# Hybrid attention block on one core: transposes of the probabilities issued in groups

## The chip, the cores and the metric

One Trainium2 chip, one of its cores. The metric is device time in microseconds (us) of one execution of the kernel, as the median of several executions.

## The reference

One layer of a decoder on a sequence of 512 rows of width 1024, in float32. The input is normalised to `h`; one wide product `h @ w_in` gives queries, keys, values and gates of two attention branches, and the columns of two merge gates.

- Differential attention, 4 heads: two score matrices of 512 x 512 per head (64 wide each), causal mask, softmax on each, and the weights `a0 - lam * a1` times values 128 wide; then an RMS norm and a SiLU gate.
- MoBA attention, 8 heads of 64; with blocks of 256 and a top-3 of at most two blocks it is plain causal softmax attention here, followed by a SiLU gate.

```python
a = jax.nn.softmax(s, axis=-1)
w = a[:, :, 0] - lam * a[:, :, 1]
return jnp.einsum('bhqk,bkhe->bqhe', w.astype(v.dtype), v)
```

Both branches are projected to 1024, merged by sigmoid gates, projected once more and added to `x`; a gated per-layer embedding is added, and a last RMS norm gives the output.

## The kernel before, in words

Every float32 product is made of three (or two) products of a rounded high part and a rest: `hi` is made by ScalarE (ACT) with a copy, `lo` by a subtraction `src - hi` on VectorE (DVE) or GpSimd (POOL). `mm3` (L114) issues the three matmuls.

**The clock of the program.** The order of the instructions on every engine is written out by a small scheduler that runs while the kernel is built. `tick` (L68) advances a counter and resumes every running generator whose time has come, the oldest first. `spawn` (L65) adds a generator, with `after` ticks of delay; a generator that yields `n` sleeps for `n` ticks. The long matrix products call `step` (L213) after each group of matmuls on TensorE (PE): three matmuls of 512 columns in `proj_T`, six of 256 columns in `proj_v`. So one tick is about one group of matmuls, and what the generators issue in a tick lands in the instruction streams between two such groups. Engines run their own streams in order and wait on semaphores for each other; a tick fixes places in the streams, not times.

**The heads.** For `j` from 0 to 7 the loop at L605 computes values (`proj_v`, 8 ticks), then `project(j)`: keys, queries and gate of pair `j`, 8 ticks each, and spawns `attention` for them two ticks later. `j` 0 to 3 are the differential heads (`kind` 0), `j` 4 to 7 hold two MoBA heads each (`kind` 1). So the attention of head `j` is issued in the middle of the products of head `j + 1`. Counted from the end of `project(j)`, the key product of the next head ends with tick 16, its query product with tick 24, its gate product with tick 32, and the next attention starts at tick 34.

**Attention.** `PLAN` (L35) is a list of steps by hand for the four query tiles of 128 rows: `S` issues the score matmuls (L482, L484) into two banks of PSUM, `E` the masked maximum on DVE (L492) and the exponentials on ACT (L497), `N` the normalisation on DVE (L502 and L534, L535, or L532), `T` the transposes of the normalised probabilities on PE (L508); a number is a sleep in ticks. For tile `i` there are `i + 1` blocks of 128 x 128 to transpose, into one bank of the tag `tp` (two banks, taken in turn). One tick later ACT copies the tile's transposed blocks to `pth`, and again one tick later DVE computes `ptl` (both by `split_later`, L102 and L104). After the last tile the product with the values is issued: L566 to L568 with `mm3` for a differential head (bank `av`), L557 to L560 for the MoBA pair. For a differential head there follow the square on ACT (L572), the gate product `o` on DVE (L573), row sums (L577) and a broadcast of the norm (L583).

With the ticks counted as above, a plan begins at tick 2 and reaches `T0` (with `S3`) at tick 9, `T1` at 15, `N3` at 19, `T2` at 20, `T3` at 24 and the product with the values at 29.

**What stands beside it.** When the key product of the next head has ended, `qk_tile` (L432) begins at tick 17: four operations of rotary embedding on DVE (L435 to L438), at tick 21 two copies to `ks` on ACT (L443), at 22 two more to the other half (L447), at 23 two subtractions to `kl` on DVE (L454), at 24 two copies of them (L458). For the queries the same begins at tick 25 with the four operations on DVE; the copies to `qs` (L443) come at tick 29 and the two subtractions to `qs` (L454) at tick 31, behind L573 of the head before. The next head's first scores (L482) read `qs`. Weights are split by `pump_split` (L179) every third tick: the copy `wh` or `vh` on ACT (L102), `wl` or `vl` on POOL (L104).

Of the kernel before, what the change touches and what calls it, by code (L numbers as in the profile page):

```python
# [9 lines left out]
F32 = mybir.dt.float32  # L10
F32R = mybir.dt.float32r
I32 = mybir.dt.int32
AF = mybir.ActivationFunctionType
ALU = mybir.AluOpType

P = 128
S = 512
D = 1024
NT = S // P
# [12 lines left out]
PUMP = 3  # L32
AV_LAG = 1
BUFS = dict(w=3, v=2)
PLAN = "S0 E0 2 S1 1 E1 1 N0 S2 3 E2 N1 T0 S3 5 E3 1 N2 T1 4 N3 1 T2 4 T3 5"  # L35
SUB_LAG = (2, 3, 1, 2, 3)
C_DQ, C_DK, C_DV, C_DG, C_MQ, C_MK, C_MV, C_MG, C_GA, C_GB = (
    0, 512, 1024, 1536, 2048, 2560, 3072, 3584, 4096, 5120)
# [3 lines left out]
def hybrid_block(ctx, tc, x, p, norm_g, w_in, lq1, lk1, lq2, lk2, subln_g, w_bd, w_bm,  # L42
                 w_out, w_ple, w_pg, final_g, rope, out):
    nc = tc.nc
    V, A, G, T, Y = nc.vector, nc.scalar, nc.gpsimd, nc.tensor, nc.sync
# [12 lines left out]
    def bank(tag):  # L58
        return ps.tile([P, 512], F32, tag=tag, name=tag, bufs=BANKS[tag])
# [5 lines left out]
    def spawn(gen, after=0):  # L65
        running.append([clock[0] + after, gen])
# [34 lines left out]
    def split_later(hi, lo, src, gap=1, eng=None):  # L101
        A.activation(hi, src, AF.Copy)  # L102
        yield gap
        (eng or V).tensor_sub(lo, src, hi.bitcast(F32))  # L104

    def pow_half(ssum, n, eps, cols):

        v = small.tile([P, cols], F32, name=f"rv{cols}")
        y = small.tile([P, cols], F32, name=f"ry{cols}")
        V.tensor_scalar(v, ssum, 1.0 / n, eps, op0=ALU.mult, op1=ALU.add)  # L110
        G.tensor_tensor(out=y, in0=v, in1=mhalf[:, :cols], op=ALU.pow)  # L111
        return y

    def mm3(acc, ahi, alo, bhi, blo, start, stop):  # L114
        T.matmul(acc, ahi, bhi, start=start, stop=False)  # L115
        T.matmul(acc, ahi, blo, start=False, stop=False)  # L116
        T.matmul(acc, alo, bhi, start=False, stop=stop)  # L117
# [156 lines left out]
    with tc.tile_pool(name="norm", bufs=2) as npool:  # L274
# [32 lines left out]
        pts = [bank("tp") for _ in range(2)]  # L307
# [194 lines left out]
            V.reciprocal(self.rc, self.sm)  # L502
            return self.rc

    def p_transposed(e, i):
        acc = bank("tp")
        for kb in range(i + 1):
            T.transpose(acc[:, kb * P:(kb + 1) * P], e[:, kb * P:(kb + 1) * P], ident)  # L508
        return acc[:, :(i + 1) * P].rearrange("p (k q) -> p k q", q=P)

    def pt_tiles():

        return (att.tile([P, 13 * P], F32R, name="pth"), att.tile([P, 13 * P], F32R, name="ptl"))

    def pt_q(pt, i):
        v = pt.rearrange("p (b q) -> p b q", q=P)
        return v[:, i:4 * i + 1:3]

    def pt_k(pt, kb):
        return pt[:, 4 * kb * P:(3 * kb + NT) * P]  # L520

    def attention(kind, j, qkg, v):

        q, k, g = qkg
        sm = [Softmax(q, k, i) for i in range(NT)]
        pts = [pt_tiles() for _ in range(1 + kind)]

        def norm(i):
            e, rc = sm[i].e, sm[i].recip()
            if kind:  # L530
                for s in range(2):
                    V.tensor_scalar(e[s], e[s], rc[:, s:s + 1], 0.5, op0=ALU.mult, op1=ALU.mult)  # L532
            else:
                V.tensor_scalar(e[1], e[1], rc[:, 1:2], nlam, op0=ALU.mult, op1=ALU.mult)  # L534
                V.scalar_tensor_tensor(e[0], e[0], rc[:, 0:1], e[1], op0=ALU.mult, op1=ALU.add)  # L535

        def trans(i):
            for s in range(1 + kind):
                acc = p_transposed(sm[i].e[s], i)
                spawn(split_later(pt_q(pts[s][0], i), pt_q(pts[s][1], i), acc), after=1)  # L540

        for op in PLAN.split():
            if op[0] == "S":
                sm[int(op[1])].scores()
            elif op[0] == "E":
                sm[int(op[1])].exps()
            elif op[0] == "N":
                norm(int(op[1]))
            elif op[0] == "T":
                trans(int(op[1]))  # L550
            else:
                yield int(op)
        if kind:
            for s in range(2):
                acc = bank(("av", "tp")[s])
                vp = v.rearrange("p (t h e) -> p t h e", t=NT, h=4)[:, :, 2 * (j % 2) + s]
                for kb in range(NT):  # L557
                    for n in range(2):
                        T.matmul(acc[:, kb * P:], vp[:, kb], pt_k(pts[s][n], kb), start=kb == 0 and n == 0,
                                 stop=kb == NT - 1 and n == 1)  # L560
                spawn(moba_out(j, s, acc, g[0], sm[3].e[s]), after=1)
                yield AV_LAG
            return
        acc = bank("av")
        vp = v.rearrange("p (t h n e) -> p t h n e", t=NT, h=2, n=2)[:, :, j % 2]
        for kb in range(NT):  # L566
            mm3(acc[:, kb * P:], vp[:, kb, 0], vp[:, kb, 1], pt_k(pts[0][0], kb), pt_k(pts[0][1], kb),
                kb == 0, kb == NT - 1)  # L568
        yield SUB_LAG[0]

        sq = sm[3].e[0]
        A.activation(sq, acc, AF.Square)  # L572
        V.scalar_tensor_tensor(oraw[j], acc, gsub, g[0], op0=ALU.mult, op1=ALU.mult)  # L573
        yield SUB_LAG[1]
        tot = bank("tp")
        for i in range(NT):
            T.matmul(tot[:, 2 * i:2 * i + 2], sq[:, i * P:(i + 1) * P], ones, start=True, stop=True)  # L577
        yield SUB_LAG[2]
        rstd = pow_half(tot[:, 0:2 * NT:2], P, SUBLN_EPS, NT)
        yield SUB_LAG[3]  # L580
        rb = bank("tp")
        for i in range(NT):
            T.transpose(rb[:, i * P:(i + 1) * P], rstd[:, i:i + 1].to_broadcast([P, P]), ident)  # L583
        yield SUB_LAG[4]
        V.tensor_mul(oraw[j], oraw[j], rb)

    def moba_out(j, s, acc, g, tmp):
        own, other = slice(s * HD, (s + 1) * HD), slice((1 - s) * HD, (2 - s) * HD)
        A.activation(tmp[own], acc[other], AF.Copy)
        yield 1  # L590
        V.tensor_add(tmp[own], acc[own], tmp[own])
        G.tensor_mul(oraw[4 + j][own], tmp[own], g[own])
# [12 lines left out]
    for j in range(7):  # L605
        if j:
            h = (j + 1) // 2
            if j % 2:
                vs.append(v_tile())
            proj_v(vs[h], h // 2, h % 2, (0, 1) if j % 2 else (2, 3))  # L610
        spawn(attention(j // 4, j % 4, project(j), vs[j // 2]), after=2)
    acc = bank("pj")
    proj_T(acc, ("a", 0))
    A.activation(oraw[7], acc, AF.Copy)
    spawn(attention(1, 3, project(7), vs[3]), after=2)

    first = [ropet[:, 0], ropet[:, 1]]
    acc = bank("pj")  # L620
# [49 lines left out]
    for m in range(3, 8):  # L670
        sig = []
        for n in range(2):
            acc = bank(("pj", "sc")[n])
# [183 lines left out]
```

## Time and profile before

| | us |
|---|---|
| median of 3 runs | 493.42 (493.4 to 493.52) |
| profiled execution | 493.49 |
| its span, first to last instruction | 491.3 |
| PE busy / DVE / ACT / POOL | 479.3 / 294.2 / 244.2 / 118.2 |
| instructions | 6677 |

The profiled execution takes 2.2 us beside its span, and it is 0.07 us above the median. The mean granted TensorE clock is 0.997 of full speed. Busy time of PE is the union of its instructions, and matmuls overlap, so the distance between two starts tells more than a duration: in a steady stream a matmul of 512 columns starts 0.23 us after the one before.

### The profile page before, as it was taken

The page shows a single profiled execution, that of the slowest core. Times are in us where ns is not written, and L with a number is a line of the kernel's source. Part 1 is how long each engine was busy: PE and PEld are TensorE (multiplying, and loading weights), DVE is VectorE, ACT ScalarE, POOL GpSimd, SP SyncE. Part 2 cuts the span into 40 slices and gives each one's busy share as a digit, 9 for nine tenths or more (in the row PEclk, how much of TensorE's full clock was granted, in tenths as well). Part 3 has the DMA queues.
Part 4 walks back from the last instruction along what each step waited for, and adds up shares of the span by engine and source line. Part 5 has one row for each costly group of instructions (what it writes and reads, how often), then busy time and mean ns, then how long its engine had stood idle before and what let it go on. Part 6 is the DMA issues. An engine that isn't in the chain of part 4 may idle for free.

```text
span 491.3 us, 6677 instructions
## 1 busy us (share of the span) xinstructions
PE 479.3 (98%) x2485; PEld 408.1 (83%) x2485; DVE 294.2 (60%) x626; ACT 244.2 (50%) x521; POOL 118.2 (24%) x104
## 2 busy tenths in 40 slices
PE   7999999999999999999999999999999999999994
PEld 5898988889888898988888887888888888888884
DVE  3775685877858668677686547642354245353565
ACT  3865755575645657556676545422332232332442
POOL 1105543542344423425456440000000000000001
PEclk9999999999999999999999999999999999999998
DMA  8954331232114311211323312423322293200013
GB/s 266 340 177 128 97 119 44 85 97 76 45 43 121 94 45 43 87 31 57 87 86 102 113 45 85 129 85 87 128 86 87 88 326 100 85 1 0 1 43 128
DMA packets 63007, 47.73 MB, mean 97 GB/s; under 512 B 2304, under 2 KB 56320, under 8 KB 62976
## 3 DMA queue, kind: packets, MB, share of 16 engines
q1 hardware_dynamic: 62832, 47.06, 31.3%
q8 instruction: 19, 0.31, 0.3%
q10 hardware_dynamic: 144, 0.26, 0.1%
q14 instruction: 12, 0.10, 0.1%
HBM read 45.22 MB, written 2.10 MB: 96 GB/s over the span
## 4 chain that ended last, share of the span: by engine, by line
PE 84%; DVE 9%; ACT 2%; issue 1%; DMA 1%; SPq 0%; POOL 0%; POOLq 0%; DVEq 0%; ACTq 0%
PE pj L115 15%; PE pj L117 14%; PE pj L116 14%; PE sc L115 4%; PE sc L116 4%; PE sc L117 4%; PE av L116 3%; PE tp L115 3%; PE tp L116 3%; PE tp L117 3%; PE av L117 3%; PE av L115 3%; PE sc L484 2%; PE sc L482 2%; DVE ptl L104 2%; PE tp L508 2%
## 5 line engine op out<-in xcount | busy, mean ns | idle before, releaser
L104 POOL TENSOR_TENSOR wl<-raw,wh 128x512 fp32r<-128x512 f32 x54 | 71.7, 1342 | 96.9 <-ACT wh L102 96.6
L115 PE MATMUL pj<-hThi,wh 128*128 128x512 f32 x232 | 93.0, 401 | 0.0
L117 PE MATMUL pj<-hThi,wl 128*128 128x512 f32 x232 | 90.8, 392 | 0.0
L116 PE MATMUL pj<-hTlo,wh 128*128 128x512 f32 x232 | 90.6, 390 | 0.0
L102 ACT ACTIVATE wh<-raw 128x512 fp32r<-128x512 f32 x96 | 56.8, 623 | 20.1 <-PE tp L117 17.2
L111 POOL TENSOR_TENSOR ry<-rv,mhalf 128x1 f32<-128x1 f32 (+1 forms) x11 | 8.2, 742 | 233.4 <-DVE rv L110 233.4
L497 ACT ACTIVATE sc<-sc,nm 128x128 f32<-128x128 f32 (+3 forms) x64 | 35.5, 556 | 33.2 <-DVE nm L492 33.2
L117 PEld LDWEIGHTS pj<-hThi,wl 128*128 128x128 f32 x232 | 43.6, 188 | 9.5
L104 DVE TENSOR_TENSOR wl<-raw,wh 128x512 fp32r<-128x512 f32 x42 | 27.8, 687 | 38.7 <-ACT wh L102 38.5
L116 PEld LDWEIGHTS pj<-hTlo,wh 128*128 128x128 f32 x232 | 43.7, 188 | 7.9
L115 PEld LDWEIGHTS pj<-hThi,wh 128*128 128x128 f32 x232 | 43.7, 188 | 7.8
L115 PE MATMUL pj<-vh,hThi 128*128 128x256 f32 (+1 forms) x136 | 39.8, 293 | 0.0
L492 DVE CUSTOM_DVE_ANT_0 sc<-sc,mask 128x128 f32<-128x128 f32 (+3 forms) x64 | 28.8, 487 | 18.4 <-PE sc L484 18.4
L117 PE MATMUL pj<-vh,hTlo 128*128 128x256 f32 (+1 forms) x136 | 39.0, 287 | 0.0
L116 PE MATMUL pj<-vl,hThi 128*128 128x256 f32 (+1 forms) x136 | 39.0, 287 | 0.0
L104 DVE TENSOR_TENSOR ptl<-tp,pth 128x128 fp32r<-128x128 f32 (+3 forms) x48 | 22.0, 486 | 23.9 <-ACT pth L102 23.8
L104 DVE TENSOR_TENSOR vl<-raw,vh 128x512 fp32r<-128x512 f32 x28 | 18.6, 687 | 29.0 <-ACT vh L102 29.0
L102 ACT ACTIVATE vh<-raw 128x512 fp32r<-128x512 f32 x48 | 28.4, 626 | 12.9 <-issue 8.6
L104 POOL TENSOR_TENSOR vl<-raw,vh 128x512 fp32r<-128x512 f32 x20 | 25.9, 1307 | 25.6 <-ACT vh L102 25.6
L102 ACT ACTIVATE pth<-tp 128x128 fp32r<-128x128 f32 (+3 forms) x48 | 19.0, 430 | 16.9 <-PE tp L508 16.7
L116 PEld LDWEIGHTS pj<-vl,hThi 128*128 128x128 f32 x136 | 25.9, 191 | 0.5
L115 PEld LDWEIGHTS pj<-vh,hThi 128*128 128x128 f32 x136 | 25.9, 190 | 0.5
(285 smaller groups left out, 1066.7 us busy)
## 6 DMA issues: line engine op xcount, KB each, us to landing
raw<-in_w_in_dram SPq DMA_DIRECT2D x48, 512.0 KB, 3.9
raw<-in_w_out_dram SPq DMA_DIRECT2D x8, 512.0 KB, 3.8
raw<-in_w_ple_gate_dram SPq DMA_DIRECT2D x8, 512.0 KB, 3.7
xt<-in_x_dram SPq DMA_DIRECT2D x4, 512.0 KB, 8.5
raw<-in_w_branch_diff_dram SPq DMA_DIRECT2D x8, 256.0 KB, 2.9
raw<-in_w_branch_moba_dram SPq DMA_DIRECT2D x8, 256.0 KB, 3.2
xs<-in_x_dram SPq DMA_DIRECT2D x1, 2048.0 KB, 10.8
out_dram<-o SPq DMA_DIRECT2D x3, 512.0 KB, 2.6
```

Of the source, the lines that this page charges most:

```text
L102: A.activation(hi, src, AF.Copy)
L104: (eng or V).tensor_sub(lo, src, hi.bitcast(F32))
L111: G.tensor_tensor(out=y, in0=v, in1=mhalf[:, :cols], op=ALU.pow)
L115: T.matmul(acc, ahi, bhi, start=start, stop=False)
L116: T.matmul(acc, ahi, blo, start=False, stop=False)
L117: T.matmul(acc, alo, bhi, start=False, stop=stop)
L482: T.matmul(self.accs[s][:, :kv], qs_[:, s, qs], ks_[:, s, :kv], start=True, stop=False)
L484: T.matmul(self.accs[s][:, :kv], qs_[:, s, qs], kl[:, s, :kv], start=False, stop=True)
L492: V.tensor_tensor_reduce(out=self.e[s], in0=self.accs[s][:, :kv], in1=mask[:, 384 - i * P:384 - i * P + kv], op0=ALU.add, op1=ALU.min, sca ...
L497: A.activation(self.e[s], self.e[s], AF.Exp, bias=self.nm[:, s:s + 1], scale=-1.0, accum_out=self.sm[:, s:s + 1])
L508: T.transpose(acc[:, kb * P:(kb + 1) * P], e[:, kb * P:(kb + 1) * P], ident)
```

## The change

The transposes of tiles 0 and 1 are issued together (`T01`), at the place of `T1`, into one bank: three blocks. For differential heads tiles 2 and 3 are issued together as well (`T23`), at tick 23, that is three ticks after the old place of `T2` and one before that of `T3`. Their seven blocks are more than the four that fit in a bank, so each of the two gets a bank of its own. The copies of a bank's tiles are issued in one tick, their subtractions in the next. MoBA pairs keep `T2` and `T3` where they were. The product with the values stays at tick 29. The number of instructions is the same; a differential head takes three banks for its transposes instead of four, a MoBA pair six instead of eight.

```diff
-PLAN = "S0 E0 2 S1 1 E1 1 N0 S2 3 E2 N1 T0 S3 5 E3 1 N2 T1 4 N3 1 T2 4 T3 5"
+PLAN = ("S0 E0 2 S1 1 E1 1 N0 S2 3 E2 N1 S3 5 E3 1 N2 T01 4 N3 4 T23 6",
+        "S0 E0 2 S1 1 E1 1 N0 S2 3 E2 N1 S3 5 E3 1 N2 T01 4 N3 1 T2 4 T3 5")
...
-    def p_transposed(e, i):
-        acc = bank("tp")
+    def p_transposed(acc, e, i):
+
         for kb in range(i + 1):
...
+        def split_tiles(s, tiles):
+            for i, acc in tiles:
+                A.activation(pt_q(pts[s][0], i), acc, AF.Copy)
+            yield 1
+            for i, acc in tiles:
+                V.tensor_sub(pt_q(pts[s][1], i), acc, pt_q(pts[s][0], i).bitcast(F32))
+
-        def trans(i):
+        def trans(*group):
+
             for s in range(1 + kind):
-                acc = p_transposed(sm[i].e[s], i)
-                spawn(split_later(pt_q(pts[s][0], i), pt_q(pts[s][1], i), acc), after=1)
-
-        for op in PLAN.split():
+                acc, at, tiles = bank("tp"), 0, []
+                for i in group:
+                    if at + i + 1 > NT:
+                        spawn(split_tiles(s, tiles), after=1)
+                        acc, at, tiles = bank("tp"), 0, []
+                    tiles.append((i, p_transposed(acc[:, at * P:], sm[i].e[s], i)))
+                    at += i + 1
+                spawn(split_tiles(s, tiles), after=1)
+
+        for op in PLAN[kind].split():
...
-                trans(int(op[1]))
+                trans(*map(int, op[1:]))
```

## Rows read from the trace of the kernel before

**Rows 1.** The page, busy time by engine.
```profile
PE 479.3 (98%) x2485; PEld 408.1 (83%) x2485; DVE 294.2 (60%) x626; ACT 244.2 (50%) x521; POOL 118.2 (24%) x104
```
**Rows 2.** The waits: waiter, releaser, us in total, times, longest.
```profile
PEld av L116 <- DVE ptl L104: 2.6, 4, 0.8
```
**Rows 3.** Timeline of PE: start, us, instruction; `T2` of head 0, `T3` of head 4.
```profile
68.91 0.49 PE L508 MATMUL tp<-ident,sc 128*128 128x128 f32 x3
...
69.48 0.39 PE L116 MATMUL pj<-hTlo,wh 128*128 128x512 f32 x1
69.71 0.40 PE L117 MATMUL pj<-hThi,wl 128*128 128x512 f32 x1
...
191.22 1.04 PE L508 MATMUL tp<-ident,sc 128*128 128x128 f32 x8
...
192.33 0.40 PE L116 MATMUL pj<-hTlo,wh 128*128 128x512 f32 x1
```
**Rows 4.** Timeline of PE: value product's first matmul and the next product's, heads 0, 1.
```profile
75.88 0.39 PE L115 MATMUL av<-pth,v 128*128 128x512 f32 x1
...
78.35 0.45 PE L115 MATMUL pj<-hThi,wh 128*128 128x512 f32 x1
...
105.63 0.39 PE L115 MATMUL av<-pth,v 128*128 128x512 f32 x1
...
107.87 0.45 PE L115 MATMUL pj<-hThi,wh 128*128 128x512 f32 x1
```
**Rows 5.** Timelines of ACT and DVE, head 1, between `T2` and the value product.
```profile
100.26 0.49 ACT L102 ACTIVATE pth<-tp 128x384 fp32r<-128x384 f32 x1
...
103.87 0.64 ACT L102 ACTIVATE wh<-raw 128x512 fp32r<-128x512 f32 x1
104.40 0.58 ACT L102 ACTIVATE pth<-tp 128x512 fp32r<-128x512 f32 x1
...
102.69 0.74 DVE L435 STREAM_SHUFFLE qr<-pj 128x512 f32<-128x512 f32 x1
...
105.40 0.68 DVE L104 TENSOR_TENSOR ptl<-tp,pth 128x512 fp32r<-128x512 f32 x1
```
**Rows 6.** Timelines of ACT, DVE and PE, head 1, up to head 2's first scores.
```profile
108.07 0.60 ACT L572 ACTIVATE sc<-av 128x512 f32<-128x512 f32 x1 [0.70 <-PE av L117]
...
108.70 0.75 DVE L573 SCALAR_TENSOR_TENSOR o<-av,gsub,gate 128x512 f32<-128x512 f32 x1 [2.62 <-ACT sc L572]
109.48 1.41 DVE L454 TENSOR_TENSOR qs<-pj,qs 64x512 fp32r<-64x512 f32 x2
...
112.23 0.42 PE L482 MATMUL sc<-ks,qs 128*128 128x128 f32 x2
```
**Rows 7.** Timelines of DVE and ACT, head 0, the same places.
```profile
60.99 0.29 DVE L104 TENSOR_TENSOR ptl<-tp,pth 128x128 fp32r<-128x128 f32 x1 [0.26 <-ACT pth L102]
...
70.19 0.75 DVE L535 SCALAR_TENSOR_TENSOR sc<-sc,rc,sc 128x512 f32<-128x512 f32 x1
...
73.16 0.75 DVE L435 STREAM_SHUFFLE qr<-pj 128x512 f32<-128x512 f32 x1
...
73.74 0.58 ACT L102 ACTIVATE pth<-tp 128x512 fp32r<-128x512 f32 x1
...
78.55 0.60 ACT L572 ACTIVATE sc<-av 128x512 f32<-128x512 f32 x1 [1.36 <-PE av L117]
```
**Rows 8.** Timelines of DVE and PE, head 4 (MoBA): subtractions of `T1`, `T3`, value product.
```profile
184.77 0.76 DVE L104 TENSOR_TENSOR ptl<-tp,pth 128x256 fp32r<-128x256 f32 x2 [2.27 <-ACT pth L102]
...
195.25 1.28 DVE L104 TENSOR_TENSOR ptl<-tp,pth 128x512 fp32r<-128x512 f32 x2
...
195.99 0.50 PE L559 MATMUL av<-ptl,v 128*128 128x512 f32 x1
```
**Rows 9.** Timelines of PE and DVE, start of the kernel: transposes and first reads.
```profile
7.32 1.11 PE L311 MATMUL tp<-ident,praw 128*128 128x128 f32 x4 [2.08 <-DMA praw<-in_p_dram]
...
8.05 1.51 DVE L366 CAST pTh<-tp 128x256 fp32r<-128x256 f32 x4 [8.05 <-PE tp L311]
```

## The prediction

> **What bounds the kernel now.** First the page's busy times: PE is busy for 98% of the span [rows 1], so only what shortens PE's own stream or removes one of its waits gains anything, and every new wait of PE costs its full length. Then the waits: the only ones of PE between the start and the merge come from the rest `ptl` of the probabilities, and it is the weight loads of the value product that show them, four times, once per differential head [rows 2]. Then the timelines of one differential head (its successor repeats it, with small differences between even and odd heads) and of one MoBA pair.
>
> **The change part by part.**
>
> *The grouping itself.* From the start of a group of transposes to the second matmul behind it, less one ordinary matmul of 0.23 us (69.48 to 69.71): three transposes take 0.57 - 0.23 = 0.34 us, eight take 192.33 - 191.22 - 0.23 = 0.88 us [rows 3]. That is 0.11 us each at either size, with nothing fixed per group. So a group of 3 or 7 takes PE what its parts took: 0.
>
> *The differential value product.* In head 0 it takes 78.35 - 75.88 = 2.47 us, in head 1 107.87 - 105.63 = 2.24 us; heads 2 and 3 repeat these [rows 4]. Without a wait it is three matmuls each of 512, 384, 256 and 128 columns: 0.23 us for the first size and about 0.1 for the last, as for a transpose [rows 3], with 0.18 and 0.12 by columns between them, 1.87 us in all. The loss is 0.60 and 0.37 us, in four heads 1.95 us. It comes from the order on DVE: the last `ptl` (tick 26) stands behind the four query operations of tick 25. With `T23` at tick 23 both subtractions are issued at tick 25 ahead of those four, since their generator is older. When would the last one be done, in head 1? ACT: the copy of tile 2 is no longer ahead of the key copies (0.39 us earlier: 0.49 less 0.1 of overlap); the weight split of 103.87 now stands behind instead of ahead (0.53 earlier); the key chain is 0.37 later (next paragraph). So tile 2's copy starts at 104.40 - 0.39 - 0.53 + 0.37 = 103.85, tile 3's at 104.24 and ends at 104.82, and `ptl` of 0.68 ends at 105.5 [rows 5]. It is needed at 105.63 + 0.23 = 105.86. In head 0, where ACT has no split there, I get 75.4 against 76.1. The wait goes in all four heads: **-1.95 us**. Its cover is 0.3 to 0.7 us.
>
> *`T01` on ACT and DVE.* Tile 0's copy and subtraction move from tick 10/11, where DVE had time, to 16/17, directly ahead of the key operations, which then run on DVE without a pause. In a differential head the subtractions begin later by the extra copy and last longer by the extra subtraction, of 0.29 us [rows 7], about 0.21 with its overlap; the copy, of the same size, I take at 0.16. Together 0.37 us, if both subtractions wait for both copies of the bank. The trace speaks for that: DVE's gate product `o` waited 2.62 us for ACT's square, though both only read the bank [rows 6], and at the start DVE's first cast, of columns transposed long before, waited until 8.05 for transposes at 7.32 into other columns of the bank [rows 9]. So waits follow banks, not columns. The Trainium skill has the rule behind it (PSUM — Partial Sum Buffer, "PSUM bank collisions raise a hardware error"): guard a bank, not an address, because two engines on different columns of one bank collide too. The trace agrees in both rows; by columns the shift would be about 0.15 us in place of 0.37.
>
> *MoBA.* Four copies and four subtractions in place of two each (one pair: 0.76 us at `T1` [rows 8]). The transposes begin 0.22 us earlier, as `T0` no longer precedes `S3`, but a bank is complete only after three; I get the key operations starting 0.45 us later (between 0.1, by columns, and 0.5). From there DVE and ACT hand each other the chain of keys, `T2` and queries up to `ptl` of `T3`, 195.25 to 195.9, and the value product starts its second matmul at 195.99 [rows 8]: nothing in between absorbs it. Pairs 4, 5 and 6 have this; pair 7 has no next queries. 3 x 0.45 = **+1.35 us**.
>
> *The new wait: the query operations.* They now stand behind both subtractions, and these behind the key copies. In head 1 they start at 105.45 instead of 102.69 [rows 5]: 2.76 us late. Behind them in order: `qs` copies, a split, the square on ACT, `o` and the subtractions to `qs` on DVE. Of the lateness the square absorbs 0.70 us, which ACT waited for PE; 2.06 us remain, and the subtractions end at 109.48 + 1.41 + 2.06 = 112.95 [rows 6]. Head 2's first scores were due at 112.23, now 0.37 earlier; the second of them, 0.13 later, reads the second half of `qs`: due at 111.99, with a weight load ahead of it. Wait: 1.1 us, in heads 1 and 3 **+2.2 us** (0.5 to 1.6 each, if the overlaps of 0.1 per instruction fall out more or less well). In head 0 the queries start at 75.3 instead of 73.16, 2.1 late, and the square had 1.36 us to spare [rows 7]: 0.8 remains, and the same sum leaves the scores late by 0.1 us at most.
>
> *`T3`'s input.* `N3` ended at 70.94 in head 0 [rows 7], now at 71.31. PE reaches tick 23 three groups after 68.91 [rows 3], at 70.97, and tile 3 at 71.3, its first weight load 0.15 us sooner: a wait of 0.2 us at most, which then delays the scores too instead of adding to their wait. Heads 0 and 2 together **+0.4 us**; in heads 1 and 3 the normalisation ends 0.1 sooner than needed.
>
> *Costed at nothing.* `S3` starts 0.11 us sooner, its maxima too; DVE then idles until `T1`. Banks of `tp`: each is read long before its third use. POOL's subtractions follow the splits that ACT now issues up to 2.8 us later behind `qs`; the weights are used two products on, some 11 us, so only a shift of that size would show. SP's loads follow the splits, six tiles ahead. After pair 7 everything is as before.
>
> *Sum.* -1.95 + 1.35 + 2.2 + 0.4 = +2.0 us on the profiled execution's 493.49 us, which is 0.07 us above the median: 495.4 us.
>
> **The rivals.**
>
> *The query chain has more slack than I count.* If head 2's scores are never late (the lateness must shrink by 1.1 us, or the scores be later by as much), -1.95 + 1.35 + 0.4 = -0.2 is left: 493.2 us. For it: I follow seven instructions on two engines, each good to 0.1 us. Against it: DVE's order is fixed by the program, and the idle time in rows 6 is what it is.
>
> *The waits follow columns.* Then `T01` shifts the keys by 0.15 us, MoBA's product by 0.1 to 0.2, the scores wait 0.85 us: -1.95 + 1.7 + 0.45 = +0.2, 493.6 us. Rows 6 and 9 speak against it.
>
> *Faster: only the value product changes.* The one mechanism is the first `ptl` wait going, with slack in the keys' chain for `T01` and in the queries' chain for `T23`: -1.95 to -1.0, about 491.9 us. It decides if the subtractions to `qs` end before 111.8 in head 1, that is if the queries start less than 1.6 us late. What speaks for it is that every displaced operation runs on engines that are idle 40 to 50% of the span; what speaks against it is that DVE has no gap in the places named.
>
> *The change does not do what it says.* For tiles 2 and 3 it does not: they get two banks, merely issued together. That is in the sum.
>
> *The rule on rotating banks.* If the copies of a bank could not begin until its whole group is through, and this held up PE at the next use of the bank, each `T01` would cost up to its copies, 0.4 us, times 7: +2.8, with the value product's gain +0.9 and 494.3 us. But the bank's next use is five ticks on, 3.4 us, while the copies and subtractions end some 2 us after the group. The Trainium skill says this of independent groups (Perfetto Trace Analysis, "Optimizing Tensor Performance", Matmuls): rotate them through banks, so that one is evacuated while the next is computed. No row here shows PE waiting for a bank.
>
> **How the numbers follow.** A measurement of this kernel tells about 0.2%, 1 us, from no change. Chances: the forecast, with its own spread of 494.5 to 496.5, 0.55; more slack in the query chain 0.14; columns 0.10; faster 0.15; rotation or others 0.06. Slower by over 0.2% (above 494.4): 0.57, the forecast and a little of the last. Within 0.2%: 0.27. Faster: 0.16. The forecast's own range is 494.5 to 496.5; down to 492.5 it takes in the columns, the slack and part of the faster case, and upward it ends at 496.4, with the waits of heads 1 and 3 at 1.6 us.
>
> **What the changed kernel's profile would show.** The wait of the value product's weight loads for `ptl` should be gone from the list for L116; the twelve matmuls should take 1.9 us in all four heads. In its place PE's weight loads should wait at L482 for DVE's L454 in heads 1 and 3, about 1 us each, and DVE should stand idle for over 1 us ahead of the subtractions of `T23`, with the query operations behind. In pairs 4 to 6 the second matmul of the value product should start 0.45 us later after the first. The prediction is wrong if the scores do not wait, or if the key operations start less than 0.2 us later behind `T01`.

## The result and the profile after

The changed kernel takes **498.06 us** (median of 5 executions, 496.57 to 498.57) against 493.4 for the kernel before (5 executions, 492.74 to 493.52): ratio 1.0088, 95% interval 1.007 to 1.0106. It is slower, by 4.3 us going by the ratio and 4.7 going by the medians, where 2.0 were predicted, and outside the range given.

The profiled execution took 497.48 us, its span is 495.7 (before: 491.3), the mean granted TensorE clock 0.990 (before: 0.997). About half of that difference in clock lies at the start of the kernel (0.75 and 0.89 in the means of 5 to 10 and of 10 to 14 us, before 1.00 in both), where the change alters nothing; so what the clock costs is read below from a single stretch. In the code after, `split_tiles` copies at L540 and subtracts at L543, and every line behind the plan stands 1 to 15 lines further down than before.

The page of the changed kernel, the line that answers to [rows 1]:

```profile
PE 480.7 (97%) x2485; PEld 410.5 (83%) x2485; DVE 298.8 (60%) x626; ACT 243.3 (49%) x521; POOL 118.3 (24%) x104
```

Each engine has as many of these instructions as before (the whole program has 6685 for 6677; the eight more are semaphore instructions, which are not counted here), but DVE is busy 4.6 us longer and PE 1.4. Something holds some of the instructions up; that is the first hint. The waits of the changed kernel (waiter, releaser, us in total, times, longest), in the place of [rows 2]:

```profile
PEld tp L509 <- DVE ptl L543: 3.5, 3, 1.2
PEld av L574 <- DVE ptl L543: 2.5, 3, 0.8
PEld sc L483 <- DVE qs L455: 1.6, 4, 0.5
...
PE sc L483 <- DVE qs L455: 1.1, 4, 0.4
```

The wait of the differential value product (before: L116) is gone, as meant. The scores' wait (`sc` for `qs`) was forecast. The largest was not: three times PE's transposes wait for `ptl`, that is for a bank of `tp` to be read out, and after each the MoBA value product (L574) waits longer than before. Three are the pairs 4, 5 and 6. In the kernel before, that product had a line in the list too, which [rows 2] does not show:

```profile
PEld av L559 <- DVE ptl L104: 1.3, 3, 0.5
```

The differential value product in the changed kernel, timeline of PE, head 0, as in [rows 4]:

```profile
75.10 0.39 PE L116 MATMUL av<-pth,v 128*128 128x512 f32 x1
...
76.96 0.44 PE L116 MATMUL pj<-hThi,wh 128*128 128x512 f32 x1
```

It takes 1.86 us here and in heads 1 to 3: 0.61 and 0.38 less, 1.98 in four heads.

The scores behind head 3 in the changed kernel, timeline of PE (behind head 1 the same two waits stand):

```profile
168.60 0.95 PE L592 MATMUL tp<-ones,sc 128*128 128x2 f32 x8
169.72 0.33 PE L483 MATMUL sc<-ks,qs 128*128 128x128 f32 x1 [0.17 <-DVE qs L455]
170.45 0.33 PE L483 MATMUL sc<-ks,qs 128*128 128x128 f32 x1 [0.40 <-DVE qs L455]
...
170.83 0.34 PE L116 MATMUL pj<-vh,hThi 128*128 128x256 f32 x1
...
171.36 0.41 PE L117 MATMUL pj<-vl,hThi 128*128 128x256 f32 x1
171.58 0.42 PE L118 MATMUL pj<-vh,hTlo 128*128 128x256 f32 x1
...
175.01 0.60 PE L598 MATMUL tp<-ident,ry 128*128 128x128 f32 x4
```

and the same places in the kernel before:

```profile
170.72 0.95 PE L577 MATMUL tp<-ones,sc 128*128 128x2 f32 x8
...
172.01 0.33 PE L115 MATMUL pj<-vh,hThi 128*128 128x256 f32 x1
...
174.69 0.60 PE L583 MATMUL tp<-ident,ry 128*128 128x128 f32 x4
```

From the row sums to the first matmul behind the scores it takes 170.83 - 168.60 = 2.23 us; before it took 1.29 (172.01 - 170.72). Two such places: +1.88. Then comes something else: from 171.36 on the 256-column matmuls start every 0.215 us instead of every 0.12. The windows of that stretch (length, then busy time of PE, PEld, DVE, ACT, POOL, then the granted clock, DMA share and GB/s):

```profile
170.00:171.00 1.00, 0.60 (x5) 0.56 (x5) 0.97 (x2) 0.00 (x0) 0.00 (x0) 1.00 0.67 181
171.00:172.00 1.00, 1.00 (x7) 1.00 (x7) 0.60 (x6) 0.65 (x3) 0.32 (x1) 0.67 1.06 318
172.00:173.00 1.00, 1.00 (x6) 1.00 (x6) 0.00 (x0) 0.75 (x3) 1.00 (x2) 0.50 0.15 39
...
174.00:175.00 1.00, 1.00 (x7) 1.00 (x7) 0.96 (x6) 0.58 (x3) 1.00 (x1) 0.62 0.00 0
```

PE waits twice for `qs`, and right behind it the granted clock falls to 0.50, the 1.2 GHz level, until about 174.8. The work from 170.83 to 175.01 takes 4.18 us; the same work took 2.68 before (172.01 to 174.69). The clock costs **1.50 us** that no term of the prediction held.

Now the pairs. Timelines of DVE, POOL and PE in pair 4, first in the kernel before:

```profile
185.45 0.74 DVE L435 STREAM_SHUFFLE qr<-pj 128x512 f32<-128x512 f32 x1
...
186.69 0.94 DVE L437 TENSOR_TENSOR qr<-qr,ropet 128x512 f32<-128x512 f32 x1
...
190.17 1.02 DVE L104 TENSOR_TENSOR ptl<-tp,pth 128x384 fp32r<-128x384 f32 x2 [0.71 <-ACT pth L102]
...
185.79 2.98 POOL L104 TENSOR_TENSOR wl<-raw,wh 128x512 fp32r<-128x512 f32 x2 [9.52 <-ACT wh L102]
...
190.99 0.40 PE L117 MATMUL pj<-hThi,wl 128*128 128x512 f32 x1
```

and the same places in the changed kernel, with the copies on ACT, PE's transposes and the value product:

```profile
185.09 1.15 DVE L543 TENSOR_TENSOR ptl<-tp,pth 128x128 fp32r<-128x128 f32 x4 [3.05 <-ACT pth L540]
186.17 0.75 DVE L436 STREAM_SHUFFLE qr<-pj 128x512 f32<-128x512 f32 x1
186.81 0.69 DVE L437 TENSOR_TENSOR pj<-pj,ropet 128x512 f32<-128x512 f32 x1
187.42 1.76 DVE L438 TENSOR_TENSOR qr<-qr,ropet 128x512 f32<-128x512 f32 x1
...
191.72 1.02 DVE L543 TENSOR_TENSOR ptl<-tp,pth 128x384 fp32r<-128x384 f32 x2 [0.81 <-ACT pth L540]
...
196.80 1.28 DVE L543 TENSOR_TENSOR ptl<-tp,pth 128x512 fp32r<-128x512 f32 x2
...
189.95 1.21 ACT L444 ACTIVATE ks<-pj 64x512 fp32r<-64x512 f32 x2 [3.41 <-DVE pj L439]
191.19 0.87 ACT L540 ACTIVATE pth<-tp 128x384 fp32r<-128x384 f32 x2
...
186.10 2.54 POOL L105 TENSOR_TENSOR wl<-raw,wh 128x512 fp32r<-128x512 f32 x2 [10.91 <-ACT wh L103]
...
183.99 0.82 PE L509 MATMUL tp<-ident,sc 128*128 128x128 f32 x6
...
191.24 0.39 PE L118 MATMUL pj<-hThi,wl 128*128 128x512 f32 x1
192.33 1.12 PE L509 MATMUL tp<-ident,sc 128*128 128x128 f32 x8 [0.70 <-DVE ptl L543]
...
196.72 0.39 PE L574 MATMUL av<-pth,v 128*128 128x512 f32 x1
197.53 0.51 PE L574 MATMUL av<-ptl,v 128*128 128x512 f32 x1 [0.42 <-DVE ptl L543]
```

Read it from the top. The key operations start 0.72 us later (186.17 for 185.45). Behind the transposes PE's stream is itself 0.25 us later (191.24 for 190.99), and POOL's subtraction 0.31 (186.10 for 185.79); against either, the key operations have lost 0.4 to 0.5 us, and that is the shared bank's doing. Two of the key operations take what they took, but the multiplication of `qr` by the rotary table takes **1.76 us instead of 0.94**. It is the one whose two inputs both lie in SBUF, and it now falls beside POOL's second weight subtraction. ACT's copies to `ks` wait for the key operations, and ACT's copies of `T2` to `pth` stand behind those; so the `ptl` of `T2` begins at 191.72, where it began at 190.17. `T3` writes the two banks from which that `ptl` reads: before, the second subtraction ended at 191.19, and `T3` wrote its first bank at 191.22 [rows 3] and its second 0.44 later. That was a cover of half a microsecond. Of the 1.55 us of lateness 0.25 are PE's own (191.24 for 190.99), and the other 1.3 go through it: `T3` starts 192.33 - 191.24 = 1.09 us behind the matmul ahead of it instead of 0.23.

The bank's wait is where this lateness is paid first; by these rows it is no cost of its own. The `ptl` of `T3` is as late as that of `T2`, 196.80 for 195.25 [rows 8], and DVE comes to it without idle time. The value product needs it, so what `T3` had not waited for would have been waited for there. The 0.86 us at `T3` and the 0.36 more at the value product (1.92 for 1.56) are together about the 1.3 us by which the chain on DVE and ACT is late against PE. No run gave `T3` a bank of its own to test this.

**Where the 4.4 us of span went**, from PE's starts in the two profiled executions: the pairs 4 to 6, 2.67 us at `T3` (0.86, 0.91, 0.90) and 1.27 at the value product (1.92, 1.91, 1.92 where it took 1.56, 1.52, 1.40), together +3.94; the scores +1.88; the clock +1.50; the differential value product -1.98. That is +5.34. The start of the kernel was 0.7 us shorter in this execution (its first transposes waited 1.07 us for their DMA, before 2.08 [rows 9]; part of what that won was lost again at the lower clock named above), which is no work of the change. 0.2 us are left unplaced.

### The profile page after: what moved, and what is told of

The parts are those of the page before. It is cut to its first block, busy times and chain, and to the rows that moved or that the text cites. A ratio compares the mean times of both kernels' runs of the same rounds, so it can differ in the third digit from the quotient of the medians.

```text
span 495.7 us, 6685 instructions
## 1 busy us (share of the span) xinstructions
PE 480.7 (97%) x2485; PEld 410.5 (83%) x2485; DVE 298.8 (60%) x626; ACT 243.3 (49%) x521; POOL 118.3 (24%) x104
## 4 chain that ended last, share of the span: by engine, by line
PE 77%; DVE 12%; ACT 6%; issue 2%; DMA 1%; POOL 0%; SPq 0%; POOLq 0%; DVEq 0%; ACTq 0%
PE pj L116 13%; PE pj L117 13%; PE pj L118 13%; PE sc L116 4%; PE sc L118 4%; PE sc L117 4%; PE tp L116 3%; PE tp L117 3%; PE tp L118 3%; PE av L116 2%; PE av L117 2%; PE av L118 2%; DVE ptl L543 2%; PE sc L483 2%; PE sc L485 2%
## 5 line engine op out<-in xcount | busy, mean ns | idle before, releaser
L116 PE MATMUL pj<-hThi,wh 128*128 128x512 f32 x232 | 92.7, 400 | 0.0
L116 PEld LDWEIGHTS pj<-hThi,wh 128*128 128x128 f32 x232 | 43.7, 188 | 7.8
L116 PE MATMUL pj<-vh,hThi 128*128 128x256 f32 (+1 forms) x136 | 40.4, 297 | 0.0
L543 DVE TENSOR_TENSOR ptl<-tp,pth 128x128 fp32r<-128x128 f32 (+3 forms) x48 | 21.0, 485 | 26.8 <-ACT pth L540 26.7
L540 ACT ACTIVATE pth<-tp 128x128 fp32r<-128x128 f32 (+3 forms) x48 | 17.9, 436 | 19.9 <-PE tp L509 19.8
L116 PEld LDWEIGHTS pj<-vh,hThi 128*128 128x128 f32 x136 | 26.5, 195 | 0.5
```

Of the source, the lines that this page charges most:

```text
L540: A.activation(pt_q(pts[s][0], i), acc, AF.Copy)
L543: V.tensor_sub(pt_q(pts[s][1], i), acc, pt_q(pts[s][0], i).bitcast(F32))
```

## The experiments

To be told apart were two things. First the place: the MoBA pairs, by the bank that `T3` waits for, or the differential heads, by the scores and the clock. Then the cause of the bank's wait: the later key operations that meet POOL's subtraction, or their lateness alone, whatever POOL does. Ratios are against runs of the kernel before on the same chip, with 95% intervals; diffs are against the changed kernel unless said otherwise.

**One kind of head at a time.** Only the differential heads with the new plan:

```diff
-        "S0 E0 2 S1 1 E1 1 N0 S2 3 E2 N1 S3 5 E3 1 N2 T01 4 N3 1 T2 4 T3 5")
+        "S0 E0 2 S1 1 E1 1 N0 S2 3 E2 N1 T0 S3 5 E3 1 N2 T1 4 N3 1 T2 4 T3 5")
```

> The differential heads have the changed plan, the MoBA pairs the old one. Theory: the loss of the change is mostly in the MoBA pairs (about +4.1 us), so this kernel keeps the value product's gain (-1.95 us), pays the scores' wait in heads 1 and 3 (+1.9 us) and whatever TensorE's clock loses after those waits (1.5 us for each time it falls, none to two): 493.4 to 496.4 us, no bank wait of the MoBA transposes. Rival: the MoBA losses come from the differential heads shifting the phase of GpSimd against VectorE, then they stay: 497 us or more.

Measured: 494.13 us, ratio 1.0005 (0.9988 to 1.0022). No wait for a bank, the scores' wait stands (1.6 us of `PEld`, four times), and the clock fell here too, to 0.94 in the mean of 90 to 120 us: behind head 1, not behind head 3. What the value product gains the scores and the clock give back.

Only the MoBA pairs with the new plan:

```diff
-PLAN = ("S0 E0 2 S1 1 E1 1 N0 S2 3 E2 N1 S3 5 E3 1 N2 T01 4 N3 4 T23 6",
+PLAN = ("S0 E0 2 S1 1 E1 1 N0 S2 3 E2 N1 T0 S3 5 E3 1 N2 T1 4 N3 1 T2 4 T3 5",
```

> The MoBA pairs have the changed plan, the differential heads the old one. Theory: tiles 0 and 1 in one bank start the key operations 0.5 us later, and this brings the multiplication of qr by the rope table behind GpSimd's second subtraction (0.9 us before, 1.8 us after); the last transposes wait for a bank about 0.9 us and the value product 0.3 us more, in three pairs: +4 us, 497.4 us, granted clock as before (0.997). Rival, my prediction as it stood (only 0.45 us per pair, nothing else): 494.8 us, and the multiplication at 0.9 us.

Measured: 497.28 us, ratio 1.0072 (1.0048 to 1.0096). Its waits:

```profile
PEld tp L509 <- DVE ptl L543: 3.5, 3, 1.2
PEld av L117 <- DVE ptl L543: 2.6, 4, 0.8
PEld av L574 <- DVE ptl L543: 2.5, 3, 0.9
```

The lines of the pairs are those of the full change to a tenth, and that of the differential value product is the one of [rows 2]. In the three pairs `T3` is late by 0.85, 0.91 and 0.91 us, and the value product takes 1.91, 1.91 and 1.90: +3.9 in the trace, +3.6 (2.4 to 4.7) by the ratio. The two kernels add up to the full change (0.05% and 0.72% against 0.88%), so the loss is in the pairs.

**The differential part in halves.** `T01` alone there:

```diff
-PLAN = ("S0 E0 2 S1 1 E1 1 N0 S2 3 E2 N1 S3 5 E3 1 N2 T01 4 N3 4 T23 6",
-        "S0 E0 2 S1 1 E1 1 N0 S2 3 E2 N1 S3 5 E3 1 N2 T01 4 N3 1 T2 4 T3 5")
+PLAN = ("S0 E0 2 S1 1 E1 1 N0 S2 3 E2 N1 S3 5 E3 1 N2 T01 4 N3 1 T2 4 T3 5",
+        "S0 E0 2 S1 1 E1 1 N0 S2 3 E2 N1 T0 S3 5 E3 1 N2 T1 4 N3 1 T2 4 T3 5")
```

> Only tiles 0 and 1 of the differential heads are grouped, tiles 2 and 3 and the MoBA pairs as before. Theory: the key operations start 0.37 us later and everything behind them on VectorE with them, up to the last subtraction that the value product waits for: its wait grows from 0.60 and 0.37 by up to 0.37 us in four heads: 494.9 us; if the later start moves the multiplication out of GpSimd's way (0.69 instead of 1.04 us), the two cancel and it stays at 493.4. Rival: grouping in one bank is free: 493.4 with the multiplication unchanged.

Measured: 493.73 us, ratio 1.0004 (0.9988 to 1.0021). Timelines of DVE and POOL, head 0:

```profile
67.98 0.68 DVE L438 TENSOR_TENSOR qr<-qr,ropet 128x512 f32<-128x512 f32 x1
...
66.81 2.99 POOL L105 TENSOR_TENSOR wl<-raw,wh 128x512 fp32r<-128x512 f32 x2 [3.40 <-ACT wh L103]
```

and in the kernel before:

```profile
67.68 1.04 DVE L437 TENSOR_TENSOR qr<-qr,ropet 128x512 f32<-128x512 f32 x1
...
66.88 2.99 POOL L104 TENSOR_TENSOR wl<-raw,wh 128x512 fp32r<-128x512 f32 x2 [3.45 <-ACT wh L102]
```

The same lateness that lengthens the multiplication in a pair shortens it in a differential head, from 1.04 to 0.68 us: it now comes 1.17 us after POOL's start, when the first of the two subtractions is nearly through, and POOL's second gives way, as it did before (2.99 us for the two in both). The shift is paid back nearly on the spot: the value product's weight loads wait 3.1 us in all, for 2.6 before.

`T23` alone there:

```diff
-PLAN = ("S0 E0 2 S1 1 E1 1 N0 S2 3 E2 N1 S3 5 E3 1 N2 T01 4 N3 4 T23 6",
-        "S0 E0 2 S1 1 E1 1 N0 S2 3 E2 N1 S3 5 E3 1 N2 T01 4 N3 1 T2 4 T3 5")
+PLAN = ("S0 E0 2 S1 1 E1 1 N0 S2 3 E2 N1 T0 S3 5 E3 1 N2 T1 4 N3 4 T23 6",
+        "S0 E0 2 S1 1 E1 1 N0 S2 3 E2 N1 T0 S3 5 E3 1 N2 T1 4 N3 1 T2 4 T3 5")
```

> Only tiles 2 and 3 of the differential heads are issued together, tiles 0 and 1 and the MoBA pairs as before. Theory: the value product's wait goes (-1.95 us), the scores of heads 2 and 4 still wait, 0.6 to 0.9 us each as the query operations start over 2 us late: 492.7 to 493.3 us if the clock stays, 1.5 us more for each time it falls. Rival: it is the lateness from tiles 0 and 1 that makes the scores wait: 491.5 us, no wait at the scores.

Measured: 492.59 us, ratio 0.9978 (0.9962 to 0.9994). The value product's wait is gone; the scores wait once per place (0.8 us of PE in all, two times, behind heads 1 and 3), and the clock did not fall behind them. This half of the change gains by itself.

**POOL out of the way in the pairs.** The kernel with the new plan in the pairs alone, and there, while the keys are worked on, no subtraction by POOL: ACT makes the high part and, one tick later, a copy of the raw weights in the place of their rest. Every instruction of DVE and PE stays. `beside[0]` holds the tick at which the projections of a pair ended. Diff against the kernel with the new plan in the pairs alone:

```diff
+        beside_keys = beside[0] is not None and 12 <= clock[0] - beside[0] <= 20
...
-            yield from split_later(hi[:, ks], lo[:, ks], src, LO_LAG, lo_engine[0])
+            if beside_keys:
+                A.activation(hi[:, ks], src, AF.Copy)
+                yield 1
+                A.activation(lo[:, ks], src, AF.Copy)
+            else:
+                yield from split_later(hi[:, ks], lo[:, ks], src, LO_LAG, lo_engine[0])
...
```

> The kernel with only the MoBA pairs changed, but the weight rests that GpSimd subtracts beside the key operations of these pairs are copied by ScalarE from the raw weights instead (so these rests hold the wrong values, and GpSimd has nothing to do there). Theory: without GpSimd beside it the multiplication of qr by the rope table takes 0.68 us instead of 1.8, the key operations end 0.2 us later than before the change instead of 1.3, the bank wait of the last transposes goes and the value product waits at most 0.3 us more per pair: 493.4 to 494.5 us. Rival: it is the shared bank and the two extra copies alone that make the transposes wait: the wait stays over half a us per pair and the time above 496 us.

Measured: 494.97 us, ratio 1.0039 (1.0023 to 1.0055). The multiplication takes 0.68 us again, but `T3` still waits for 0.40 and 0.46 us in pairs 4 and 5 (not in 6). The reason is the experiment's own: its second copy on ACT stands ahead of the copies to `pth`. So once more without the tick between the two:

```diff
-                yield 1
```

> As the run without GpSimd beside the key operations, but ScalarE's substitute copy follows its first copy at once, so that it no longer stands between the key copies and the copies of the third query tile, where it cost 0.63 us (the weight rests concerned again hold raw weights). Theory: what was left of the bank wait in that run (0.4 us in pairs 4 and 5, none in pair 6) came from that copy; without it no bank wait in any pair, and the value product waits 0.2 to 0.3 us more per pair than before: 493.9 us, +0.1 to +0.2%. Rival: the shared bank of tiles 0 and 1 makes the last transposes wait by itself: wait of 0.4 us and 495 us as in that run.

Measured: 493.73 us, ratio 1.0016 (1.0004 to 1.0028). Timelines of DVE and PE, pair 4:

```profile
185.82 0.74 DVE L442 STREAM_SHUFFLE qr<-pj 128x512 f32<-128x512 f32 x1
...
187.06 0.68 DVE L444 TENSOR_TENSOR qr<-qr,ropet 128x512 f32<-128x512 f32 x1
...
190.27 1.02 DVE L549 TENSOR_TENSOR ptl<-tp,pth 128x384 fp32r<-128x384 f32 x2 [0.82 <-ACT pth L546]
...
191.14 1.04 PE L515 MATMUL tp<-ident,sc 128*128 128x128 f32 x8
```

`T01` is as in the full change, the keys start as late behind it, POOL is away, and `T3` follows its matmul after 0.23 us in all three pairs. Of 3.6 us, 0.8 (0.2 to 1.4) are left, and the trace has them at the value product: 1.76, 1.81 and 1.81 us for 1.56, 1.52 and 1.40. The lateness alone does not make the bank's wait; with POOL it does.

**The multiplication ahead of its neighbour.** If the order on DVE is turned so that the SBUF multiplication comes first, it reaches POOL's first subtraction and not its second. Diff against the kernel with the new plan in the pairs alone:

```diff
-        V.tensor_mul(acc, acc, ropet[:, 0])
         V.tensor_mul(r, r, ropet[:, 1])
+        V.tensor_mul(acc, acc, ropet[:, 0])
```

> The kernel with only the MoBA pairs changed, with the two rotary multiplications in the other order everywhere: qr by the rope table first, then pj. Theory: the multiplication of qr comes 0.6 us sooner, meets GpSimd's first subtraction instead of its second and waits 0.6 us less in pairs 4 to 6: its duration 1.1 to 1.2 us instead of 1.8, the bank wait 0.3 us instead of 0.9, about 495.3 us. Rival: VectorE's delay does not depend on what GpSimd is doing at that moment: 497.3 us.

Measured: 498.75 us, ratio 1.0109 (1.0086 to 1.0132), over 3 us above what was expected. Its list of waits:

```profile
PEld av L117 <- DVE ptl L543: 4.6, 4, 1.4
...
PEld tp L509 <- DVE ptl L543: 1.5, 3, 0.5
```

and its timelines of DVE and POOL, the multiplication in head 0 and in pair 4:

```profile
68.68 1.51 DVE L437 TENSOR_TENSOR qr<-qr,ropet 128x512 f32<-128x512 f32 x1
...
190.61 0.99 DVE L437 TENSOR_TENSOR qr<-qr,ropet 128x512 f32<-128x512 f32 x1
...
68.35 2.99 POOL L105 TENSOR_TENSOR wl<-raw,wh 128x512 fp32r<-128x512 f32 x2 [3.43 <-ACT wh L103]
...
189.76 2.99 POOL L105 TENSOR_TENSOR wl<-raw,wh 128x512 fp32r<-128x512 f32 x2 [9.53 <-ACT wh L103]
```

In the pairs the multiplication did about what was expected of it, 0.99 us, and the bank's wait fell from 3.5 to 1.5. But the order was turned everywhere, and in the differential heads the multiplication now came 0.33 us after POOL's start and took 1.51 us; their value product waited 4.6 us instead of 2.6. By PE's starts the four differential value products took 2.45 us longer than in the run with the pairs alone, and that of pair 6 took 2.29 us instead of 1.90. So most of the miss is one more case of the mechanism it was to test.

**What a good order gives.** The old places of the tiles, and the value product one tick later, with the square left at its tick (one behind the product instead of two):

```diff
-PLAN = ("S0 E0 2 S1 1 E1 1 N0 S2 3 E2 N1 S3 5 E3 1 N2 T01 4 N3 4 T23 6",
-        "S0 E0 2 S1 1 E1 1 N0 S2 3 E2 N1 S3 5 E3 1 N2 T01 4 N3 1 T2 4 T3 5")
-SUB_LAG = (2, 3, 1, 2, 3)
+PLAN = ("S0 E0 2 S1 1 E1 1 N0 S2 3 E2 N1 T0 S3 5 E3 1 N2 T1 4 N3 1 T2 4 T3 6",
+        "S0 E0 2 S1 1 E1 1 N0 S2 3 E2 N1 T0 S3 5 E3 1 N2 T1 4 N3 1 T2 4 T3 6")
+SUB_LAG = (1, 3, 1, 2, 3)
```

> The kernel before with one more tick between the last transposes and the value product, for both kinds (T3 6 in place of T3 5), and one tick less behind it for the differential heads (SUB_LAG 1 in place of 2), nothing grouped. Theory: the value product's wait is a matter of its place alone; it goes in all seven places (0.60 and 0.37 twice each, 0.35, 0.30 and 0.17) with the query operations where they were, so no wait at the scores: 2.8 us faster, 490.6 us. Rival: the wait is only moved behind the value product, to the square and the next scores: 493 us.

Measured: 491.06 us, ratio 0.9952 (0.9935 to 0.9968). No wait for `ptl` or `qs` is left in the heads. It beats both kernels; the wait that the change meant to remove goes by a later consumer, with no earlier producer.

`T23` alone as in its own run above, with the square and `o` a tick later, behind the subtractions to `qs`, and the row sums where they were (diff against that run's kernel):

```diff
-SUB_LAG = (2, 3, 1, 2, 3)
+SUB_LAG = (3, 2, 1, 2, 3)
```

> Only tiles 2 and 3 of the differential heads issued together (as in the run of that alone), and in addition the square and the gate product one tick later (SUB_LAG 3, 2 in place of 2, 3), so that they stand behind the subtractions to qs. Theory: the subtractions to qs then start 1.4 us sooner, the wait of the scores of heads 2 and 4 goes, and TensorE's clock with nothing to fall after: 1.5 us less than with tiles 2 and 3 alone, 491.2 us. Rival: the copies to qs themselves are what is late: 492.6 us.

Measured: 491.13 us, ratio 0.996 (0.9945 to 0.9975): the scores do not wait. With the pairs' value product a tick later as well:

```diff
-        "S0 E0 2 S1 1 E1 1 N0 S2 3 E2 N1 T0 S3 5 E3 1 N2 T1 4 N3 1 T2 4 T3 5")
+        "S0 E0 2 S1 1 E1 1 N0 S2 3 E2 N1 T0 S3 5 E3 1 N2 T1 4 N3 1 T2 4 T3 6")
```

> The kernel of the run before, and the MoBA pairs with one more tick ahead of the value product (T3 6). Theory: another 0.8 us from the MoBA pairs: 490.4 us; the same as the kernel with only the value product a tick later, within 0.2%. Rival: the MoBA value product ends the pair later and the next scores wait: no gain.

Measured: 490.85 us, ratio 0.9951 (0.9932 to 0.9971), not to be told from the two before it.

The full change with the later square, that is without the scores' wait:

```diff
-SUB_LAG = (2, 3, 1, 2, 3)
+SUB_LAG = (3, 2, 1, 2, 3)
```

> The changed kernel in full, with the square and the gate product one tick later (SUB_LAG 3, 2 in place of 2, 3). Theory: the scores' wait in heads 2 and 4 goes (1.0 us each) and with it the falls of TensorE's clock behind it (1.5 us each time); the MoBA pairs' 4 us stay: 495 to 496 us, 0.4 to 0.6% slower than before instead of 0.9%. Rival: the copies to qs alone are too late in the full change, as its query operations start later than with tiles 2 and 3 alone: 498 us.

Measured: 495.4 us, ratio 1.0042 (1.0025 to 1.0059). The scores' wait is gone, the granted clock is 1.00 in every stretch from 60 to 300 us, and the bank's wait stands:

```profile
PEld tp L509 <- DVE ptl L543: 3.4, 3, 1.2
PEld av L574 <- DVE ptl L543: 2.6, 3, 0.9
```

So the scores' wait and the clock behind it are worth 0.46% of the full change's 0.88%, some 2.3 us (1.0 to 3.5 by the two intervals; the profiled execution of the full change has 1.88 and 1.50), about the 2.0 that the differential value product gained.

## Why the prediction was wrong in its size

*The list of waits: a line short.* The prediction read [rows 2] as the only waits of PE between the start and the merge. The MoBA value product had three more, 1.3 us in all (L559); nothing in the sum rests on their absence.

*The value product: right.* -1.95 predicted, -1.98 in the trace. (The prediction's prices for the four sizes add up to 1.89 us and not 1.87; 1.86 was measured.) The subtractions of `T23` ahead of the query operations are in time in all four heads.

*The query chain and the scores: right.* 1.1 us each predicted behind heads 1 and 3, 0.94 measured. The path was the one named: `qs` late, on the second score matmul above all (0.40 us idle against 0.17).

*`T01`'s shift: right, by banks.* In head 0 the key operations start at 66.07 instead of 66.43 in a stream that runs 0.71 us ahead: 0.35 us late, against 0.37 by banks and 0.15 by columns. [rows 6] could not tell the two apart, since the square and `o` read the same columns. The changed kernel can: both copies of the bank are through at 65.49, and the first subtraction starts at 65.52. So the rule of the Trainium skill that the prediction leaned on (PSUM — Partial Sum Buffer, "PSUM bank collisions raise a hardware error") agrees with the trace here too, as far as the program's waits go. In the pairs the keys start 2.18 us after `T01` began, before 1.52 after `T1`; less the 0.22 us that the two transposes of `T0` take in it, 0.44 late for 0.45.

*`T3`'s input: wrong, small.* 0.4 us predicted, none measured: the seven transposes of `T23` run without idle time.

*MoBA: the step that failed.* +1.35 was predicted, +3.94 measured. The path was right: "nothing in between absorbs it" was true. The lateness itself, 0.45 us per pair, was mis-sized, because something in between adds to it. The bank's shift came as forecast (0.44), but the multiplication beside POOL takes 0.82, 0.90 and 1.01 us longer in the three pairs (1.76, 1.79 and 1.77 for 0.94, 0.89 and 0.76), which the sum had at nothing. Three times 0.44 and these make 4.05 us, for 3.94 measured.

Two lines of the paragraph on what costs nothing were wrong. **"POOL's subtractions"** were looked at only as work that could come late for its own readers, not as work beside which DVE slows down. The trace of before had it: `qr` by `ropet` took 0.94 us in pair 4 and 1.04 in head 0, and 0.68 where no subtraction of POOL was under way (at 193.92). No line of the prediction takes up that surplus. And **"each is read long before its third use"**, with "No row here shows PE waiting for a bank", was worked out for the bank of `T01`, used again five ticks on. `T2`'s banks are used again by `T3` after four, and the reading of [rows 3] beside `T2`'s subtractions would have given the slack: 191.66 - 191.19 = 0.47 us. A shift of 0.44 would just have fitted into that; 1.3 did not. The rival on rotating banks had the right resource at the wrong group. But the bank decided only where the lateness was paid; its amount came from POOL.

The run without POOL speaks for the term itself. Its value products lose 0.20, 0.29 and 0.41 us, 0.9 in all, with multiplications shorter by 0.26, 0.21 and 0.08 than before (0.94, 0.89, 0.76 to 0.68). Add these 0.55 back, and the lateness alone costs an estimated 1.45 us for 1.35.

*The clock: left out.* 1.50 us behind one of the two scores' waits. New waits of PE were charged at their length alone.

Neither of the two signs that the prediction gave for being wrong came true: the scores wait, and the key operations are late. Both tested terms that it had named; what it missed lay in a term put at nothing and in one that was not there.

How POOL and DVE exclude each other can be read off seven pairs of rows. Let DVE's SBUF multiplication come `a` us after the first of POOL's two subtractions begins:

| kernel, place | `a` | DVE takes | DVE ends after POOL's start | POOL's two take |
|---|---|---|---|---|
| multiplication first, head 0 | 0.33 | 1.51 | 1.84 | 2.99 |
| before, head 0 | 0.80 | 1.04 | 1.84 | 2.99 |
| multiplication first, pair 4 | 0.85 | 0.99 | 1.84 | 2.99 |
| before, pair 4 | 0.90 | 0.94 | 1.84 | 2.98 |
| `T01` in differential heads, head 0 | 1.17 | 0.68 | 1.85 | 2.99 |
| after, pair 4 | 1.32 | 1.76 | 3.08 | 2.54 |
| new plan in the pairs alone, pair 4 | 1.32 | 1.77 | 3.09 | 2.54 |

Whenever it comes within the first subtraction, it ends at 1.84: it waits for that one, goes in between, and POOL's second pays (2.99 for 2.54). If it comes when the second has begun, it waits for that as well and ends at 3.09. 0.15 us of lateness at this point cost 1.24. The Trainium skill has the rule (SBUF — State Buffer, "Summary: rules for kernel authors"): a DVE operation with two SBUF inputs and a GpSimd operation that reads SBUF shut each other out, and the one that is issued second waits for the whole of the first. The table agrees, and so do the neighbours: the multiplication of `pj`, which reads one input from PSUM, takes 0.69 to 0.70 us beside POOL's subtraction (186.81 in pair 4 after).

What stays open: what sets the clock's fall off, and why it fell behind only one of two waits that look alike, behind head 3 in the full change and behind head 1 in the run of the differential heads alone.

## What to carry to other kernels

Before an operation is moved on VectorE, look at what GpSimd does at its new place, and compare the durations of the same instruction at different places of the trace of before: where one form takes 0.68 us here and 1.04 there, a collision lies behind it that a shift of some tenths can remove or double. For every buffer that is used in rotation, take the slack from its tightest pair of uses, not from a typical one: it tells where a lateness will show first. If a consumer waits for the end of a chain, try the consumer one step later before the chain is rebuilt: here that gave 2.4 us, where the rebuilt chain lost more than 4.

## What the runs showed of the hardware

A lateness of a tenth can have a price of a whole instruction of another engine: the table's step from 1.84 to 3.09 us lies between arrivals of 1.17 and 1.32 us. Short of that step a lateness can be absorbed: `T01` in the differential heads was nearly free, because its shift used up the 0.36 us for which the multiplication of head 0 had waited before (1.04 for 0.68), and it ended 1.84 us behind POOL's start before and 1.85 with the shift.

PE's clock can be a cost of short waits too. Behind two waits with 0.17 and 0.40 us of visible idle time the granted clock went from 1.00 to 0.50, from about 171.3 to 174.8 us, at a price of 1.50, more than both; behind the twin of this place, with the same idle time, it stayed at 1.00. In the thirteen traces it fell between 60 and 300 us only behind such a double wait, once in each of the two kernels that have it. A single longer idle time did not bring it down: 0.70 us ahead of `T3` in the changed kernel, 1.0 us in a value product of the run with the turned order. So that the waits set the fall off is likely, but not shown.
